# A streaming encoder layer on one core: the prompt's state products of the scan as fp32r passes with exchanged operands, and the norm products one weight half further on

## The chip, the core and the metric

The kernel runs on one core of a Trainium2 chip. The metric is the device time in microseconds of one execution; lower is better. Everything is fp32 in and out. The engines are called by their short names in the profile: PE is TensorE (matrix products; PEld is its weight load), DVE is VectorE, ACT is ScalarE, POOL is GpSimd and SP is SyncE, which issues most of the transfers.

## The reference, cut to what matters

One layer is computed for 256 frames of a new stream (the prompt) and for 8 running streams of 16 frames (the sample), 384 tokens together. The layer projects the normed input, runs a pooling branch and a Mamba-2 scan (SSD), merges them by gates, and ends with an MLP. The change lies in the scan, in the state that the scan leaves behind:

```python
y = jnp.einsum('btsgr,bsgrp->btgrp', cb[..., None] * decay, xdt)
y = y + jnp.einsum('btgn,bgrpn->btgrp', Cc, h) * jnp.exp(cum)[..., None]
last = cum[:, -1]
w_end = jnp.exp(last[:, None] - cum)
h = h * jnp.exp(last)[..., None, None] + jnp.einsum('bsgn,bsgr,bsgrp->bgrpn', Bc, w_end, xdt)
...
h = h * lax.rsqrt(jnp.mean(h * h, axis=-1, keepdims=True) + EPS)
```

There are 8 groups (g) of 8 heads of 64 channels, and a state of 128 per channel. For the prompt, whose state starts at zero, the state is a sum over all 256 frames of B times the weighted input: for each pair of heads, 128 channels by 128 states, summed over two blocks of 128 frames. It is an output (new_ssm_p). The last line is that of gated_rmsnorm, over a group's 512 channels.

## The kernel before, in words

**Arithmetic.** Most products are made of fp32r passes: each operand is split into a high part (a rounded copy, by ScalarE) and a low part (the rest, by VectorE), and three products, high by high, high by low and low by high, are summed in PSUM (mm3, L161; wsplit, L73). Products written on fp32 tiles show in the profile as two passes each.

**Weights.** The large projections run through flow (L121). Its list items holds weight halves: 1024 columns of a weight matrix, fetched by SP four halves ahead (fetch), split by ScalarE and VectorE two or three halves ahead (prep), and used in 24 products of 384 columns each (half, L166). Between halves stand calls, added by at(...), that do the scan's own work. Each engine executes its instructions in the order in which the program lists them.

**The work list.** Smaller work of VectorE and ScalarE is put in a list with a cost and a name (later, L88). After each half, work (L91) takes entries worth 2.6 from the front; need (L99) takes entries until the named ones are done.

**A block** (block, L592) belongs to half a group, so there are 16 of them plus a last call. It finishes the half group before it (old) and starts the next (new). For old, PE computes the outputs Y from the decayed products E (L603), adds the sample's part (L632), and computes the prompt's state pp: for each of two head pairs and two blocks of frames, one fp32 product with the weighted input xdw as weights and B (Bk) as the moving operand, 128 columns (L636). For new, PE computes the sample's input from its old state (yi, L623), transposes the inputs (trx, L643) and, in the first half of a group, B (trB, L648) and the products of C and B (cb, L651). The results lie in six PSUM banks, which are taken as others come free. VectorE then reads yi (yis, L655), Y (xs, L665) and trx (xdt, xdw, L676), ScalarE copies pp to pe (L667), and POOL stores it with two transfers (L669). In the first half of a group, ScalarE copies trB's prompt part to Bk (L684) and the sample's part is split into Bhl (L686, L687) and stored to b_scr (L688).

**The sample's state.** state_tasks (L717) splits the sample's third of xdw into xhl (L723, L724) and stores it to x_scr (L725). SP then loads the old state hs (L575) and reads b_scr and x_scr back in another layout: bst (L824) and xst (L833). update (L838) uses them for the su products, 256 columns in fp32r (L846).

**The norm.** gated_tasks (L729) sums the squares of a group in ssum and splits the sum into sh (ScalarE, L749) and sl (VectorE, L750). norm_mm (L791) sums them over the channels with two fp32r products bc_g (L795, L796) against ones, and puts the following steps of VectorE in the work list.

**The order by hand** (L869 to L907 for each group): B and C with the second update of the group before, three projections of x, a block, the fourth x, the transfers, z0, the first half of z1, an update, the second half of z1, norm_mm of the group before, z2, z3, a block, and a gate (gate_units, L553). At the end (L940 to L952) come the remaining gates with the last block, whose pp stands in the block, and the last norm. PE waits at a half whose weights are not split yet.

## Time and profile before

| what | value |
| --- | --- |
| three runs, median | 2798.02 us (2796.97 to 2801.68) |
| the profiled execution, its own time | 2799.5 us |
| its span, from the first to the last instruction | 2797.7 us |
| granted TensorE clock, mean | 0.998 |

The profile lists the engines' busy times, the chain that ended last, groups of instructions by line, waits and a timeline. In a timeline row stand the start in us from the span's start, the duration, the engine, the line, the operation, the tile written and the tiles read, the shapes, the count, and in brackets how long the engine had been idle before and what ended that. Matrix products overlap, so the pace of PE is read from start to start, not from a row's duration.

### The profile page before, as it was taken

To read this page: it belongs to the slowest core of one execution; us is meant where nothing else is said; L and a number is where in the kernel's file an instruction comes from. 1 tells how busy PE (TensorE), PEld (TensorE's weight loads), DVE (VectorE), ACT (ScalarE), POOL (GpSimd) and SP (SyncE) were. 2 spreads that over 40 slices of the span, in tenths; PEclk is the share of its full clock that TensorE was granted. 3 is DMA by queue.
4 is the path that set the end of the run, shared out by engine and by line. 5 is a ranking of instruction groups with operands and counts; after the bars stand their busy time and mean duration, and the time that the engine had idled before them with its cause. 6 is when DMAs were issued, how large, how long until landed. Compare 5 with 4: busy or idle time off the path is not lost.

```text
span 2797.7 us, 40260 instructions
## 1 busy us (share of the span) xinstructions
PE 2784.7 (100%) x15964; PEld 2656.5 (95%) x15964; DVE 1766.9 (63%) x2217; ACT 1323.5 (47%) x2076; POOL 191.0 (7%) x295
## 2 busy tenths in 40 slices
PE   9999999999999999999999999999999999999998
PEld 9999999999999999999999988999999999999997
DVE  8774334567667767667633334666767667676766
ACT  6443223555555554554422223545555555555553
POOL 0000000000000000001000000000111111111111
PEclk9999999999999999999999999999999999999999
DMA  6444445556556556555744454445666566666656
GB/s 223 134 134 139 138 141 171 191 170 216 193 181 209 197 183 208 199 184 186 263 158 155 151 200 132 153 165 185 179 162 166 162 161 163 176 177 186 183 125 249
DMA packets 161468, 492.89 MB, mean 176 GB/s; under 512 B 20032, under 2 KB 43392, under 8 KB 156416
## 3 DMA queue, kind: packets, MB, share of 16 engines
q1 hardware_dynamic: 133008, 406.07, 43.1%
q0 software_dynamic: 28128, 84.24, 12.6%
q8 instruction: 125, 2.05, 0.3%
q14 instruction: 63, 0.52, 0.1%
q10 hardware_dynamic: 144, 0.01, 0.0%
HBM read 412.35 MB, written 77.89 MB: 175 GB/s over the span
## 4 chain that ended last, share of the span: by engine, by line
PE 94%; DVE 2%; DMA 1%; ACT 1%; issue 1%; SPq 0%; DVEq 0%; ACTq 0%
PE pj_up L162 6%; PE pj_up L163 6%; PE pj_up L164 6%; PE pj_x L162 4%; PE pj_x L163 4%; PE pj_x L164 4%; PE wd L1410 3%; PE pj_sp L162 3%; PE wd L1411 3%; PE wd L1412 3%; PE pj_sp L164 3%; PE pj_sp L163 3%; PE pj_z L163 3%; PE pj_z L164 3%; PE pj_z L162 3%; PE t L1412 2%
## 5 line engine op out<-in xcount | busy, mean ns | idle before, releaser
L162 PE MATMUL pj_up<-x1h,wh_up 128*128 128x384 f32 x992 | 334.6, 337 | 0.0
L163 PE MATMUL pj_up<-x1l,wh_up 128*128 128x384 f32 x992 | 333.7, 336 | 0.0
L164 PE MATMUL pj_up<-x1h,wl_up 128*128 128x384 f32 x992 | 333.7, 336 | 0.0
L162 PE MATMUL pj_x<-xgh,wh_x 128*128 128x384 f32 x768 | 257.6, 335 | 0.0
L164 PE MATMUL pj_x<-xgh,wl_x 128*128 128x384 f32 x768 | 256.9, 335 | 0.0
L163 PE MATMUL pj_x<-xgl,wh_x 128*128 128x384 f32 x768 | 256.9, 335 | 0.0
L78 DVE TENSOR_TENSOR wl_wd<-raw,wh_wd 128x1024 fp32r<-128x1024 f32 x168 | 201.8, 1223 | 62.7 <-ACT wh_wd L77 59.0
L77 ACT ACTIVATE wh_wd<-raw 128x1024 fp32r<-128x1024 f32 x168 | 174.2, 1053 | 84.5 <-PE pj_up L163 42.1
L162 PEld LDWEIGHTS pj_up<-x1h,wh_up 128*128 128x128 f32 x992 | 186.9, 188 | 4.5
L163 PEld LDWEIGHTS pj_up<-x1l,wh_up 128*128 128x128 f32 x992 | 186.9, 188 | 4.5
L164 PEld LDWEIGHTS pj_up<-x1h,wl_up 128*128 128x128 f32 x992 | 186.9, 188 | 0.0
L164 PE MATMUL pj_z<-xgh,wl_z 128*128 128x384 f32 x512 | 171.3, 335 | 0.0
L162 PE MATMUL pj_z<-xgh,wh_z 128*128 128x384 f32 x512 | 171.3, 335 | 0.0
L163 PE MATMUL pj_z<-xgl,wh_z 128*128 128x384 f32 x512 | 171.3, 335 | 0.0
L162 PE MATMUL pj_sp<-abh,wh_sp 128*128 128x384 f32 x512 | 171.2, 334 | 0.0
L164 PE MATMUL pj_sp<-abh,wl_sp 128*128 128x384 f32 x512 | 171.2, 334 | 0.0
L163 PE MATMUL pj_sp<-abl,wh_sp 128*128 128x384 f32 x512 | 171.2, 334 | 0.0
L78 DVE TENSOR_TENSOR wl_sp<-w_sp,wh_sp 128x1024 fp32r<-128x1024 f32 x64 | 78.4, 1226 | 110.7 <-ACT wh_sp L77 110.7
L162 PEld LDWEIGHTS pj_x<-xgh,wh_x 128*128 128x128 f32 x768 | 144.3, 188 | 0.0
L163 PEld LDWEIGHTS pj_x<-xgl,wh_x 128*128 128x128 f32 x768 | 144.3, 188 | 0.0
L164 PEld LDWEIGHTS pj_x<-xgh,wl_x 128*128 128x128 f32 x768 | 144.2, 188 | 0.0
L78 DVE TENSOR_TENSOR wl_x<-w_x,wh_x 128x1024 fp32r<-128x1024 f32 x72 | 87.4, 1221 | 81.3 <-ACT wh_x L77 81.3
(388 smaller groups left out, 7094.2 us busy)
## 6 DMA issues: line engine op xcount, KB each, us to landing
w_up<-w_up SPq DMA_DIRECT2D x126, 512.0 KB, 4.6
raw<-w_down SPq DMA_DIRECT2D x112, 512.0 KB, 7.1
w_x<-w_in SPq DMA_DIRECT2D x96, 512.0 KB, 4.0
w_z<-w_in SPq DMA_DIRECT2D x64, 512.0 KB, 4.5
w_sp<-w_ssd SPq DMA_DIRECT2D x64, 512.0 KB, 4.7
acc_scr<-ev POOLq DMA_DIRECT2D x126, 256.0 KB, 4.4
w_ga<-w_in SPq DMA_DIRECT2D x32, 512.0 KB, 3.4
w_pp<-w_pp SPq DMA_DIRECT2D x32, 512.0 KB, 3.4
```

What stands on the lines that cost most here:

```text
L77: s.activation(h, w, AF.Copy)
L78: v.tensor_tensor(l, w, h.bitcast(F32), ALU.subtract)
L162: te.matmul(out, wh, xh, start=first, stop=False)
L163: te.matmul(out, wh, xl, start=False, stop=False)
L164: return te.matmul(out, wl, xh, start=False, stop=last)
L1410: te.matmul(o, ah, wh[:, c], start=first, stop=False)
L1411: te.matmul(o, ah, wl[:, c], start=False, stop=False)
L1412: te.matmul(o, al, wh[:, c], start=False, stop=fin)
```

## The change

The state products pp are no longer four fp32 products but two sets of three fp32r passes, with the operands exchanged: B is the weight, split into high and low, and the weighted input is the moving operand, for two head pairs at once (256 columns in two runs of 128). They run ahead of Y in the block, while the banks are asked for in the old order: Y, yi, pp. For that, Bk holds the high and the low part of all three thirds of B, and xhl those of all three thirds of the weighted input; the splits of Bhl and of the sample's third alone are gone. The store to x_scr becomes two transfers, one per part. The state is stored with one transfer of 256 columns in place of two of 128, in another layout that the host transposes.

The last state is taken out of the last block: its sample part is split where it was, its prompt part two weight halves later, and its products, copy and store follow after one more half, just before the last norm.

norm_mm of the other groups moves from the front of z2 to between its two halves.

Among the buffers, the copy pe uses the gates' buffer (tag gbt), of which there is now one instead of two until the tail, when the next phase's pool gives two; ms uses the buffers of the convolution (tag cacc). The scan's row of the constant table has a tile and a transfer of its own on POOL's queue (the table's other part shrinks by 408 columns), nrm moves to another pool, and two paddings change.

```diff
@@ -328,10 +328,13 @@
         half(early[4], 1, p4[1], xg)
     pha.close()
 
-    small.tile([P, 88], F32, name="pad_small")
+    small.tile([P, 80], F32, name="pad_small")
+    nrm = small.tile([P, 32], F32, name="nrm")
     tok = small.tile([P, 11, NH], F32, name="tok")
     decb = small.tile([P, NH, NB], F32, name="decb")
     with tc.tile_pool(name="phc", bufs=1, reuse_waits="tile") as pc, tc.tile_pool(name="phc2", bufs=2, reuse_waits="tile") as pc2:
+        scan = pc.tile([NH, T], F32, name="scan")
+        gp.dma_start(scan, io["cst"][:NH, C_SCAN : C_SCAN + T])
         bufs = []
         for i in range(2):
             b = pc.tile([P, 519], F32, name=f"pbuf{i}")
...
@@ -436,7 +439,7 @@
             v.scalar_tensor_tensor(out=dt, in0=q, scalar=2.0, in1=raw, op0=ALU.mult, op1=ALU.add)
             dta, we, dtw = n64("dta"), n64("we"), n64("dtw")
             v.tensor_scalar(dta, dt, nA, -1.0, ALU.mult, ALU.mult)
-            v.tensor_tensor_scan(cum, cst2[:NH, C_SCAN - C_MASK : C_SCAN - C_MASK + T], dta, 0.0, ALU.mult, ALU.add)
+            v.tensor_tensor_scan(cum, scan, dta, 0.0, ALU.mult, ALU.add)
             sy.dma_start(cum_scr, cum)
             nb = n64("nb")
             tot = pb.tile([NH, 1], F32, name="tot")
...
@@ -552,7 +554,10 @@
 
     def gate_units(n):
         def post(ps):
-            t = small.tile([P, T], F32, tag="gbt", name=f"gbt{n}", bufs=2)
+            if "pe1" in held:
+                t = held["pe1"].tile([P, T], F32, tag="gbt", name=f"gbt{n}", bufs=2)
+            else:
+                t = small.tile([P, T], F32, tag="gbt", name=f"gbt{n}", bufs=1)
             v.tensor_tensor(t, ps, rstd, ALU.mult)
             s.activation(t, t, AF.Sigmoid)
             gp.dma_start(gb_scr[n], t)
...
@@ -589,15 +594,32 @@
             ALU.mult,
         )
 
+    def state(g, hf, pp):
+        need(f"xhl{g}_{hf}")
+        d = S[g]
+        for b in range(2):
+            bh, bl = (d["Bk"][:, i, b, :] for i in range(2))
+            xh, xl = (d["xhl"][0][:, i, :, b, :] for i in range(2))
+            mm3(pp[:, : 2 * P].rearrange("p (j q) -> p j q", j=2), bh, bl, xh, xl, b == 0, b == 1)
+        return pp
+
+    def state_out(g, hf, pp):
+        pe = small.tile([P, T], F32, tag="gbt", name=f"pe{g}_{hf}", bufs=1)[:, : 2 * P]
+        s.copy(pe, pp[:, : 2 * P])
+        gp.dma_start(io["new_ssm_p"][g * 2 + hf], pe)
+
     def block(old, new):
         Y = []
         if old:
             g, hf = old
             need(f"E{g}_{hf * 2}", f"E{g}_{hf * 2 + 1}")
             d = S[g]
-            for j in (hf * 2, hf * 2 + 1):
-                y = sstile(f"Y{g}_{j}")
-                Y.append(y)
+            Y = [sstile(f"Y{g}_{j}") for j in (hf * 2, hf * 2 + 1)]
+            if new:
+                yi = sstile(f"yi{new[0]}_{new[1]}")
+                pp = sstile(f"pp{g}_{hf}")
+                state(g, hf, pp)
+            for j, y in zip((hf * 2, hf * 2 + 1), Y):
                 for sb, e0, c0, n in ((0, 0, 0, TP), (1, TP, P, P), (2, T, TP, P)):
                     for hh in range(2):
                         te.matmul(
...
@@ -616,7 +638,8 @@
                 need(f"x{32 + g2}", f"x{40 + g2}")
             need(f"x{g2 * 4 + j0}", f"x{g2 * 4 + j0 + 1}")
             hs = d2["hs"][h2]
-            yi = sstile(f"yi{g2}_{h2}")
+            if not old:
+                yi = sstile(f"yi{g2}_{h2}")
             for j2 in range(2):
                 for c in range(4):
                     for r in range(2):
...
@@ -630,10 +653,6 @@
         if old:
             for y, j2 in zip(Y, range(2)):
                 te.matmul(y[:, TP:T], d["yis"][hf][:, j2 * P : j2 * P + P], ident, start=False, stop=True, skip_group_check=True)
-            pp = sstile(f"pp{g}_{hf}")
-            for j2 in range(2):
-                for b in range(2):
-                    te.matmul(pp[:, j2 * P : j2 * P + P], d["xdw"][hf][:, j2, b, :], d["Bk"][:, b, :], start=b == 0, stop=b == 1)
         trx = []
         if new:
             for j in (j0, j0 + 1):
...
@@ -663,10 +682,8 @@
                 x = d["xs"][j]
                 i = V_DSK + g * 4 + j
                 v.scalar_tensor_tensor(out=x, in0=x, scalar=vec[:, i : i + 1], in1=y[:, :T], op0=ALU.mult, op1=ALU.add)
-            pe = pd.tile([P, 2 * P], F32, tag="pe", name=f"pe{g}_{hf}", bufs=1)
-            s.copy(pe, pp[:, : 2 * P])
-            for j2 in range(2):
-                gp.dma_start(io["new_ssm_p"][g * 4 + hf * 2 + j2], pe[:, j2 * P : j2 * P + P])
+            if new:
+                state_out(g, hf, pp)
         if new:
             xdw = d2["xdw"][h2] = pd.tile([P, 2, 3, P], F32, tag="xdw", name=f"xdw{g2}_{h2}", bufs=1)
             for j2, tr in enumerate(trx):
...
@@ -680,12 +697,11 @@
                         ALU.mult,
                     )
             if h2 == 0:
-                Bk = d2["Bk"] = pd.tile([P, 2, P], F32, tag="Bk", name=f"Bk{g2}", bufs=1)
-                s.copy(Bk.rearrange("p b n -> p (b n)"), trB[:, :TP])
-                Bhl = pd.tile([P, 2, P], F32R, tag="Bhl", name=f"Bhl{g2}", bufs=1)
-                s.activation(Bhl[:, 0, :], trB[:, TP:T], AF.Copy)
-                v.tensor_tensor(Bhl[:, 1, :], trB[:, TP:T], Bhl[:, 0, :].bitcast(F32), ALU.subtract)
-                sy.dma_start(b_scr[g2], Bhl.bitcast(F32))
+                Bk = d2["Bk"] = pd.tile([P, 2, 3, P], F32R, tag="Bk", name=f"Bk{g2}", bufs=1)
+                tb = trB[:, :T].rearrange("p (b n) -> p b n", b=3)
+                s.activation(Bk[:, 0], tb, AF.Copy)
+                v.tensor_tensor(Bk[:, 1], tb, Bk[:, 0].bitcast(F32), ALU.subtract)
+                sy.dma_start(b_scr[g2], Bk[:, :, 2, :].bitcast(F32))
                 cbm = d2["cbm"] = pd.tile([P, 512], F32, tag="cbm", name=f"cbm{g2}", bufs=1)
                 v.tensor_tensor(cbm, cb, cst2[:, :512], ALU.mult)
         if new:
...
@@ -717,14 +733,22 @@
     def state_tasks(g, hf):
         d = S[g]
 
-        def parts():
-            xhl = pd.tile([P, 2, 2, P], F32R, tag="xhl", name=f"xhl{g}_{hf}", bufs=1)
-            x = d["xdw"][hf][:, :, 2, :]
-            s.activation(xhl[:, 0], x, AF.Copy)
-            v.tensor_tensor(xhl[:, 1], x, xhl[:, 0].bitcast(F32), ALU.subtract)
-            sy.dma_start(x_scr[g * 2 + hf], xhl.bitcast(F32))
-
-        later(0.5, f"xhl{g}_{hf}", parts)
+        def parts(b):
+            if "xhl" not in d or d["xhl"][1] != hf:
+                d["xhl"] = pd.tile([P, 2, 2, 3, P], F32R, tag="xhl", name=f"xhl{g}_{hf}", bufs=1), hf
+            xhl = d["xhl"][0]
+            x = d["xdw"][hf][:, :, b, :]
+            s.activation(xhl[:, 0, :, b, :], x, AF.Copy)
+            v.tensor_tensor(xhl[:, 1, :, b, :], x, xhl[:, 0, :, b, :].bitcast(F32), ALU.subtract)
+            if b.stop == 3:
+                for i in range(2):
+                    sy.dma_start(x_scr[g * 2 + hf][:, i], xhl[:, i, :, 2, :].bitcast(F32))
+
+        if (g, hf) != (G - 1, 1):
+            later(0.5, f"xhl{g}_{hf}", lambda: parts(slice(0, 3)))
+            return
+        later(0.5, f"xhl{g}_{hf}", lambda: parts(slice(2, 3)))
+        held["parts"] = lambda: parts(slice(0, 2))
 
     def gated_tasks(g, hf):
         d = S[g]
...
@@ -794,7 +818,7 @@
         bc = sstile(f"bc_g{g}")[:, :T]
         te.matmul(bc, onesr, d["sh"], start=True, stop=False)
         te.matmul(bc, onesr, d["sl"], start=False, stop=True)
-        ms = pd.tile([P, T], F32, tag="ms", name=f"ms_g{g}", bufs=1)
+        ms = pd.tile([P, T], F32, tag="cacc", name=f"ms_g{g}")
         y = pd.tile([P, T], F32, tag="ssum", name=f"nwy_g{g}", bufs=1)
         a = pd.tile([P, T], F32, tag="ysq", name=f"nwa_g{g}", bufs=1)
 
...
@@ -893,9 +917,11 @@
         items += u[:1]
         at(update, g, 0)
         items += u[1:]
+        u = z_units(g, 2)
+        items += u[:1]
         if g:
             at(norm_mm, g - 1)
-        items += z_units(g, 2)
+        items += u[1:]
         u = z_units(g, 3)
         items += u[:1]
         at(cbc_load, g, 1)
...
@@ -945,7 +971,10 @@
     items += tail_[4:5]
     at(block, (G - 1, 1), None)
     at(narrow)
-    items += tail_[5:8]
+    items += tail_[5:7]
+    at(lambda: held["parts"]())
+    items += tail_[7:8]
+    at(lambda: state_out(G - 1, 1, state(G - 1, 1, sstile(f"pp{G - 1}_1"))))
     at(norm_mm, G - 1)
     items += tail_[8:11]
     at(branch_open)
```

More of the change, by code (lines that the diff above doesn't have):

```diff
@@ L228, in build @@
     rstd = small.tile([P, T], F32, name="rstd")
-    cst2 = small.tile([P, C_END - C_MASK], F32, name="cst2")
+    cst2 = small.tile([P, C_SCAN - C_MASK], F32, name="cst2")
     xg, xr = [None] * KD, [None] * KD
@@ L308, in build @@
         sy.dma_start(cst[:, :C_MASK], io["cst"][:, :C_MASK])
-        sy.dma_start(cst2, io["cst"][:, C_MASK:])
+        sy.dma_start(cst2, io["cst"][:, C_MASK:C_SCAN])
         f4 = [wfetch(win[5, q], f"p4_{q}") for q in range(2)]
@@ L508, in build @@
     s.activation(onesr, ones, AF.Copy)
-    nrm = pd1.tile([P, 32], F32, name="nrm")
     v.tensor_scalar(nrm, vec[:, V_NRM : V_NRM + 32], -1.0 / 8192.0, None, ALU.mult)
-    pd1.tile([P, 64], F32, name="pad_phd")
+    pd1.tile([P, 96], F32, name="pad_phd")
     seg = lambda a: a.rearrange("p (b t) -> p b t", b=24)
-    ncv = [0]
+    ncv, held = [0], {}
     def proj_units(ui, name, post):
@@ L907, in build @@
                 items += gate_units(gates.pop(0))
-    ab, ms_, held = [], [], {}
+    ab, ms_ = [], []
     AR = 7
@@ L1684 @@
         "new_conv": (P, 48, 9, 3),
-        "new_ssm_p": (32, P, P),
+        "new_ssm_p": (16, P, 2 * P),
         "new_ssm_s": (16, P, NB, 2 * P),
@@ L1697 @@
     nconv = r["new_conv"].transpose(2, 3, 1, 0).reshape(9, 3, 6144)
+    nsp = r["new_ssm_p"].reshape(16, P, 2, P).transpose(0, 2, 3, 1)
     nss = r["new_ssm_s"].reshape(16, P, NB, 4, 64).transpose(2, 0, 3, 4, 1).reshape(1, NB, NH, 64, P)
@@ L1704 @@
         c(nconv[:1].reshape(1, 1, 3, 6144)),
-        c(r["new_ssm_p"].reshape(1, 1, NH, 64, P)),
+        c(nsp.reshape(1, 1, NH, 64, P)),
         c(npool[1:].reshape(1, NB, 15, DM)),
```

## The prediction, made before the changed kernel ran

> **What bounds the kernel now.** I read the page first, for the engines' busy time and the chain that ended last, and then the windows view for the stretch from 490 to 1362 us, in which the scan's blocks lie.
>
> ```profile
> PE 2784.7 (100%) x15964; PEld 2656.5 (95%) x15964; DVE 1766.9 (63%) x2217; ACT 1323.5 (47%) x2076; POOL 191.0 (7%) x295
> PE 94%; DVE 2%; DMA 1%; ACT 1%; issue 1%; SPq 0%; DVEq 0%; ACTq 0%
> 490.00:1362.00 872.00, 871.30 (x5786) 854.65 (x5785) 619.79 (x877) 471.93 (x919) 52.41 (x96) 1.00 0.59 198
> ```
>
> The reader is to see that TensorE (PE) is the bound, over the whole span and in the changed stretch: busy 871.30 of 872.00 us, at a granted clock of 1.00. VectorE has 619.79 and ScalarE 471.93, so there is room beside PE, but both run in order and feed PE its weights. A microsecond taken from PE's stream comes off the end if PE is fed as before. I therefore count PE time from start to start, then ask which cover gets thinner.
>
> The timeline of PE, block of old group 0 and new group 1:
>
> ```profile
> 593.90 1.96 PE L603 MATMUL Y<-E,xdt 128*64 128x256 f32 x24
> ...
> 597.38 1.06 PE L636 MATMUL pp<-Bk,xdw 128*128 128x128 f32 x8
> 598.27 0.82 PE L643 MATMUL trx<-cst,xs 128*128 128x128 f32 x6
> ...
> 599.26 1.04 PE L651 MATMUL cb<-xs,xs 128*128 128x256 f32 x6
> 600.05 0.42 PE L162 MATMUL pj_x<-xgh,wh_x 128*128 128x384 f32 x1
> ```
>
> From Y's start to the next weight half are 6.15 us with no gap. The state products pp hold PE from 597.38 to 598.27, 0.89 us: four fp32 products, seen as eight passes.
>
> **State products: the new price.** The nearest row is the sample's update su: fp32r, 256 columns, other weights each time, as in the six new products.
>
> ```profile
> 516.04 1.11 PE L846 MATMUL su<-xst,bst 128*128 128x256 f32 x8
> 516.99 0.34 PE L162 MATMUL pj_z<-xgh,wh_z 128*128 128x384 f32 x1
> ```
>
> Eight take 0.95 us, 0.119 each; six take 0.71. Each of the 16 blocks saves 0.89 - 0.71 = 0.18, together **2.8 us**. No switch between fp32r and fp32 is added: the new products stand right behind an fp32r weight half, ahead of Y, and in the last block between two halves. The su row reads its moving operand in one run, the change reads two runs of 128 columns; no row here has that. Bounds: at no price 0.119 each; at the pace of pp (0.89 for 8 x 128 columns, 0.22 for 256) 1.33 a block, 0.44 more than before, a loss of 7.0 in all. I take su's row, the same type and width.
>
> The Trainium skill, TensorE: Matmul & The Clock Gate, section Back-to-back issue gap, gives N/2.4 + 2.5 ns for a product standing alone on a warm clock, which is 109 ns for 256 columns; six would be 0.65 and the saving 3.8. The trace's 0.119 is longer and decides.
>
> **Norm products.** The timeline of PE at the norms of groups 0, 1 and 2 (their last weight product, two norm products, next half), and group 6, where nothing waits; below them who ended the waits, from the view of the tile:
>
> ```profile
> 625.89 0.34 PE L164 MATMUL pj_z<-xgh,wl_z 128*128 128x384 f32 x1
> 627.03 0.34 PE L162 MATMUL pj_z<-xgh,wh_z 128*128 128x384 f32 x1
> ...
> 731.76 0.34 PE L164 MATMUL pj_z<-xgh,wl_z 128*128 128x384 f32 x1
> 733.38 0.34 PE L162 MATMUL pj_z<-xgh,wh_z 128*128 128x384 f32 x1
> ...
> 838.12 0.34 PE L164 MATMUL pj_z<-xgh,wl_z 128*128 128x384 f32 x1
> 838.88 0.34 PE L162 MATMUL pj_z<-xgh,wh_z 128*128 128x384 f32 x1
> ...
> 1259.45 0.34 PE L164 MATMUL pj_z<-xgh,wl_z 128*128 128x384 f32 x1
> 1259.98 0.33 PE L162 MATMUL pj_z<-xgh,wh_z 128*128 128x384 f32 x1
> ...
>   ACT sh L749: 1.4, 3
>   DVE sl L750: 1.1, 3
> ```
>
> The quiet case takes 0.53 us. Groups 0, 1 and 2 take 1.14, 1.62 and 0.76, so they wait 0.61, 1.09 and 0.23, **1.9 us**, for the two halves sh and sl of the sum of squares. The later groups wait hardly at all: the whole view has 2.5 us, part of it overlapped. Half a step later, PE has one more weight half to run, 24 products or about 4.16 us (627.03 to 631.19, below). sl would have to come over 4 us later than now to be waited for.
>
> Gross gain: 2.8 + 1.9 = **4.7 us**.
>
> **What is late next: the weights behind the norm.** In the timelines of VectorE and PE, the split that the half after next needs:
>
> ```profile
> 626.14 0.56 DVE L750 TENSOR_TENSOR sl<-ssum,sh 128x384 fp32r<-128x384 f32 x1 [0.59 <-ACT sh L749]
> 627.75 1.22 DVE L118 TENSOR_TENSOR wl_z<-w_z,wh_z 128x1024 fp32r<-128x1024 f32 x1
> 631.19 0.34 PE L162 MATMUL pj_z<-xgh,wh_z 128*128 128x384 f32 x1
> ...
> 734.10 1.22 DVE L78 TENSOR_TENSOR wl_z<-w_z,wh_z 128x1024 fp32r<-128x1024 f32 x1
> 737.54 0.34 PE L162 MATMUL pj_z<-xgh,wh_z 128*128 128x384 f32 x1
> ```
>
> The split ends at 628.97 and PE needs it at 631.19: a slack of 2.22, the same in group 1 (735.32 to 737.54). PE waited at the norm just before, so without that wait the slack is 2.22 - 0.61 = 1.6 in group 0, 2.22 - 1.09 = 1.1 in group 1, 2.0 in group 2, and about 2.4 in the other four.
>
> How much later does that split come? Its weights were issued by SP behind the block's own transfers, and SP waits there for xhl:
>
> ```profile
> 603.28 0.33 SPq L725 DMA_DIRECT2D x_scr<-xhl  x1
> 603.71 0.37 SPq L575 DMA_DIRECT2D hs<-ssm  x1
> 604.13 0.44 SPq L70 DMA_DIRECT2D w_z<-w_in  x1
> ...
> 613.98 2.69 SPq L833 DMA_DIRECT2D xst<-x_scr  x4
> 616.72 0.91 SPq L70 DMA_DIRECT2D w_z<-w_in  x2
> ```
>
> The x_scr store becomes two, one more issue of about 0.42 (603.71 to 604.13), and xhl is split over three times the columns. The view of groups by shape, over 490 to 1362 us, prices that:
>
> ```profile
> L724 DVE TENSOR_TENSOR xhl<-xdw,xhl 128x256 fp32r<-128x256 f32 x16 | 6.7, 416 | 0.0
> L687 DVE TENSOR_TENSOR Bhl<-trB,Bhl 128x128 fp32r<-128x128 f32 x8 | 2.2, 278 | 0.0
> ```
>
> Between xhl's 0.42 for 256 columns and the weight split's 1.22 for 1024, 768 columns come to 0.95, so +0.53. Bhl goes from 128 to 384 columns, 0.28 to the 0.56 of sl above, +0.28. With the issue, the chain is about **1.2 us later**. Against slacks of 1.6, 1.1, 2.0 and 2.4 that costs group 1 some 0.1; I take 0.3 for all groups. ScalarE's added columns (Bk and the high half of xhl) run while VectorE works through the block and cost nothing.
>
> **Other cover that gets thinner.** The old pp stood between Y's last products and trB and cb, which take banks that this block sets free. In the block of group 2:
>
> ```profile
> 704.13 1.13 DVE L665 SCALAR_TENSOR_TENSOR xs<-xs,vec,Y 128x384 f32<-128x384 f32 x2
> 704.44 0.35 ACT L667 COPY pe<-pp 128x256 f32<-128x256 f32 x1
> 705.13 1.04 PE L651 MATMUL cb<-xs,xs 128*128 128x256 f32 x6
> ```
>
> cb began at 705.13 while the second xs product ran to 705.26, so cb doesn't wait for that one; the copy of pp ended at 704.79. In the new order cb comes 0.18 earlier, at 704.95. The copy keeps its place on ScalarE, behind a SiLU, so 0.16 is left: price 0. With the bank of the second xs product it would be some 0.35 in each of seven blocks, 2.5.
>
> At the end, the copy of the last state shares one buffer with the gates and waits on ScalarE, an in-order engine, until gate 10's store has landed; behind it stands the split that PE needs two halves later.
>
> ```profile
> 1319.72 0.56 DVE L556 TENSOR_TENSOR gbt<-pj_gb,rstd 128x384 f32<-128x384 f32 x1
> 1321.13 0.54 POOL L558 DMA_DIRECT2D gb_scr<-gbt  x1 [7.73 <-ACT gbt L557]
> DMA to landing us min/median/max: 2.1/4.3/5.4
> ```
>
> Landing at the median, 1325.4, plus copy 0.4, ScalarE's split 1.05 and VectorE's 1.22 makes 1328.1; PE starts that half at about 1328.2 (two halves of 4.16 after 1319.88). So 0 to 1.1 us, once; I take 0.3. The late halves of the last xhl are split while PE runs a whole half, price 0. The last state's 16th saving is in the sum. Moving nrm, the shorter constant table, the scan row on POOL's queue and one state store in place of two lie beside PE's work in earlier stages or on POOL, busy 7%: price 0, and if the earlier stages are laid out otherwise, unknown by about 1 us either way.
>
> **Sum.** 2.8 + 1.9 - 0.3 - 0.3 = 4.1 us. The profiled execution took 2799.5 us, its span 2797.7 and 1.8 around it; it becomes 2795.4. The median of the three runs, 2798.02, lies 1.5 below the profiled one, so I predict **2794.0 us**. I call 0.2%, 5.6 us, what a measurement can tell from no change: below 2792.4 is faster, above 2803.6 slower.
>
> **Rivals.**
> - *Given back* (0.16). Bank order costs 2.5, or the chain is 2.5 us late in place of 1.2: then groups lose 0.9 + 1.4 + 0.5 + 4 x 0.1 = 3.2. For it: the slacks were read from one order of the work, and every block adds to them. Against: the issue and columns add up to 1.2. Time 2796 to 2797.
> - *Slower: the weights behind the norm* (0.13). If the chain from xhl over hs to the weights is d late, the loss is (d - 1.6) + (d - 1.1) + (d - 2.0) + 4 x (d - 2.4), positive parts only; at d = 2.7 it eats the 4.7, and at 4 it is 2.4 + 2.9 + 2.0 + 6.4 = 13.7: 2807. It decides at d above 3.5 for over 0.2%. For it: the store's runs shrink from 2 KB to 512 bytes, and hs, 1 MB, follows on the same queue. Against: xst, the reader of x_scr, is issued at 613.98, over ten microseconds after the store, so a slower landing is covered.
> - *The new passes run slow* (0.06): two-run moving operands at fp32's pace, +7.0 - 1.9: 2803. It is also the case that the change doesn't do what it says.
> - *More than forecast* (0.15). Products spaced by their columns alone, 256/384 of the 0.173 us between weight products (4.16/24), or 0.116, give 3.1; with 1.9 and no give-back 5.0, 2793.0, and scatter of 1 us in the median takes it under 2792.4. The Trainium skill's 109 ns would give 3.8 + 1.9 = 5.7: 2792.3.
> - Forecast (0.50): 2792.5 to 2796.
>
> DMA: Bandwidth & Descriptors, section Specifications, of the Trainium skill puts the least size for line rate at 512 bytes; by it the store's runs cost nothing. No row here shows such a store.
>
> **How the numbers follow.** Faster by over 0.2%: most of the "more" case and the forecast's edge, 0.20. Slower: the slow-weights case and half of the slow passes, 0.16. Within: 0.64. The range goes from 2790.5 (the "more" case less scatter) to 2803.0 (slow passes), leaving out the rest of the slower case.
>
> **What would show it.** Six state products from start to start in 0.71 us, ahead of Y, and the block at 5.97; norms with 0.53 in all groups; the split behind the norm 1.2 us later against the block's start, with PE waiting there 0.1 at most. Wrong would be: gaps before a weight half behind the norm, cb starting late, PE standing at the half after the last state.

## The result, and the profile after

The changed kernel takes **2803.68 us** (median of 9 runs, 2802.67 to 2808.46) against 2798.59 for the kernel before (9 runs): ratio 1.0021, 95% interval 1.0013 to 1.0030. The forecast was 2794.0 with a range to 2803.0, so it had the wrong sign, and the time lies 0.7 us beyond the range. The profiled execution took 2808.34 us and lies 4.7 above the median; the stages below are read from it, so their sums are those of this execution, 8.9 us over the profiled execution of the kernel before, and not of the medians, which lie 5.1 apart.

The page of the changed kernel, and the window of the scan's blocks:

```profile
PE 2786.7 (99%) x15932; PEld 2655.6 (95%) x15932; DVE 1777.7 (63%) x2218; ACT 1329.8 (47%) x2069; POOL 183.2 (7%) x280
490.00:1371.00 881.00, 873.95 (x5758) 855.71 (x5757) 629.49 (x876) 477.50 (x911) 42.92 (x80) 1.00 0.59 196
```

PE was busy in all but 0.70 us of that stretch before; now it stands for 7.05. The timeline of PE, first the new state products of the block of group 1 and what follows them, then the norm of group 1:

```profile
593.48 0.28 PE L162 MATMUL pp<-xhl,Bk 128*128 128x256 f32 x1
...
594.07 0.28 PE L164 MATMUL pp<-xhl,Bk 128*128 128x256 f32 x1
594.28 1.96 PE L625 MATMUL Y<-E,xdt 128*64 128x256 f32 x24
597.76 0.82 PE L662 MATMUL trx<-cst,xs 128*128 128x128 f32 x6
598.78 0.55 PE L667 MATMUL trB<-cst,xs 128*128 128x128 f32 x3 [0.20 <-DVE yis L674]
...
737.01 0.34 PE L819 MATMUL bc_g<-sh,onesr 128*128 128x384 f32 x1
737.18 0.34 PE L820 MATMUL bc_g<-sl,onesr 128*128 128x384 f32 x1
737.36 0.33 PE L162 MATMUL pj_z<-xgh,wh_z 128*128 128x384 f32 x1
```

What was to be gained is there. The six state products start 0.12 us apart; the last is 0.21 ahead of Y, because the switch from fp32r to fp32 (0.09) now stands behind them and no longer behind the weight half. The norm takes 0.35 us from its first product to the next half, with no gap. But trB, which followed the transposes of x after 0.66 us, now follows after 1.02 here. The waits of PE in the changed kernel, from 540 to 1290 us and from 1290 to 1400 us (us in total, times, longest):

```profile
PE trB L667 <- DVE yis L674: 5.3, 7, 1.8
...
PE pj_gb L164 <- DVE wl_gb L78: 0.9, 2, 0.4
PE pp L163 <- DVE xhl L742: 0.6, 1, 0.6
PE pj_sp L164 <- DVE wl_sp L78: 0.2, 1, 0.2
```

There are two new places: the transposes of B in every first half of a group, which wait for VectorE's yis, and the stretch behind the last block.

To add it up I compare the start of the same weight half in two traces; each column says by how much the difference to the kernel before grows in a stage (us, minus is a gain). "First-half blocks" are the seven with trB and cb, the half behind them included.

| stage | changed | e1 norm alone | e2 state alone | e4 tail | e5 taps | e6 taps, tail | e10 | e13 |
| --- | --- | --- | --- | --- | --- | --- | --- | --- |
| norms | -2.0 | -2.0 | +1.6 | -2.0 | -2.0 | -2.0 | -2.0 | -2.0 |
| eight second-half blocks | -1.5 | 0 | -1.5 | -1.5 | -1.5 | -1.5 | -1.5 | -1.5 |
| seven first-half blocks | **+9.2** | +0.5 | +3.5 | +6.8 | -0.7 | -0.9 | +6.8 | +1.9 |
| other halves of the scan | 0 | 0 | 0 | 0 | +1.9 | +1.5 | 0 | 0 |
| last block | -1.0 | +0.8 | -1.0 | -1.0 | -1.0 | -1.0 | -1.0 | -1.0 |
| last state | +1.6 | 0 | +0.7 | +0.7 | +1.3 | +0.7 | +0.7 | +0.7 |
| gates and the next loop | **+2.3** | 0 | +1.2 | 0 | +2.0 | 0 | +2.1 | +0.7 |

The first-half blocks would be 1.3 us shorter without waits (7 x 0.19, as in the other eight), so they lose some 10.5: 6.4 ahead of trB, 1.3 ahead of cb, the rest beside these, with 1.65 from a lower clock in one block (last section). Together the changed column is 8.6 of the 8.9 us by which the spans differ. Not all of it is the program's: e4 runs the same instructions up to the tail, and there the blocks lose 6.8 in place of 9.2, with waits of 5.6 and 1.3 and no lower clock. That is the scatter against which the waits of the other runs are to be held.

### The profile page after: what moved, and what is told of

The parts are those of the page before. It is cut to its first block, busy times and chain, and to the rows that moved or that the text cites. A ratio compares the mean times of both kernels' runs of the same rounds, so it can differ in the third digit from the quotient of the medians.

```text
span 2806.6 us, 40258 instructions
## 1 busy us (share of the span) xinstructions
PE 2786.7 (99%) x15932; PEld 2655.6 (95%) x15932; DVE 1777.7 (63%) x2218; ACT 1329.8 (47%) x2069; POOL 183.2 (7%) x280
## 4 chain that ended last, share of the span: by engine, by line
PE 39%; issue 34%; DVE 13%; ACT 6%; POOL 4%; DMA 3%; SPq 1%; POOLq 0%; DVEq 0%; ACTq 0%
POOL acc_scr L1407 3%; PE pj_sp L164 3%; PE pj_sp L163 3%; PE pj_sp L162 3%; DVE cacc L543 2%; PE pj_ga L164 2%; PE pj_ga L163 2%; PE pj_pp L164 2%; PE pj_pp L162 2%; PE pj_ga L162 2%; PE pj_pp L163 2%; PE wo L1111 2%; PE wo L1113 2%; PE wo L1112 2%; DVE wl_x L78 1%
## 5 line engine op out<-in xcount | busy, mean ns | idle before, releaser
L77 ACT ACTIVATE wh_wd<-raw 128x1024 fp32r<-128x1024 f32 x168 | 174.2, 1053 | 84.5 <-PE pj_up L163 42.1
```

Of the source, the lines that this page charges most:

```text
L77: s.activation(h, w, AF.Copy)
```

## The experiments

Three terms: the taps are the three multiply-adds of the convolution of one x tile on VectorE (L543); a round is what ScalarE and VectorE do for one half group; cover is the time between the end of a result and the moment at which another engine needs it.

Each block of times below: median, then that of the kernel before on the same chip, then the ratio with its interval. "Waits at trB and cb" are the seven gaps ahead of each, start to start, beyond the quiet 0.11. An execution scatters by about 2 us, so small edits are read from the traces.

### The two edits alone

e1 is the kernel before with norm_mm moved, e2 the changed kernel with it moved back:

```diff
+        u = z_units(g, 2)
+        items += u[:1]
         if g:
             at(norm_mm, g - 1)
-        items += z_units(g, 2)
+        items += u[1:]
```

> The kernel before with the norm products alone one weight half further; the state products stay fp32, behind the Y additions. Theory A (the loss of the change sits at the transposes of B, which take the bank of yi and so wait for VectorE's yis, and in the tail; both came with the state products, not with the norm): the three norm waits of 0.61, 1.09 and 0.24 us go and little is given back, 2796.7 us against 2798.6. Rival B (PE is paced by the weights or by VectorE's own chain, and whatever PE gains is waited for again at the next block): 2798.6, with new gaps ahead of the transposes of B as long as the norm waits were.

> The changed kernel with the norm products at their old place: the state products alone are changed. Theory A: the norm waits of 1.9 us come back, but PE then reaches the next block of a first half that much later, while VectorE's yis is where it was, so the waits ahead of the transposes of B in groups 2 and 3 shrink by up to as much: 2803.7 to 2804.7 us. Rival B (the state's loss is a price of its own, whatever PE's lead): 2805.6.

e1: 2797.62, before 2797.66, 0.9998 [0.9990, 1.0007]. Waits at trB and cb 0.3. The norm's 2.0 us are gained; 0.5 come back in one block, and 0.8 at the last, where the fp32 products of the last state come too early for a bank:

```profile
PE pp L636 <- DVE hs L850: 0.6, 1, 0.6
```

By the trace 0.7 us of the gain are left, which the time can't show.

e2: 2803.28, before 2797.66, 1.0019 [1.0010, 1.0028]; 0.4 under the range of theory A, 2.3 under rival B. The loss belongs to the state edit, and e2 shows its kind: in place of a gain the norms lose 1.6, the waits at trB and cb are 0.33 and 0.19 in every group, and the time is the changed kernel's. What PE doesn't wait for in one place it waits for in the other, so something else paces it.

### What trB waits for: VectorE's order

In the changed kernel, VectorE comes to yis only after the taps of the group's third x tile, which the block doesn't need. e3 holds them back until yis is issued:

```diff
+            if hold:
+                held["taps"] = taps
+                debt[0] -= 1.8
...
                 tok[:, 10, hd : hd + 4].unsqueeze(2).to_broadcast([P, 4, 64]),
                 ALU.mult,
             )
+            if "taps" in held:
+                held.pop("taps")()
```

e5 holds them back until the xs products and the copy of the last state are issued too:

```diff
             if new:
                 state_out(g, hf, pp)
+                if "taps" in held:
+                    held.pop("taps")()
```

> The changed kernel with one edit of VectorE's order: in the blocks of a first half the three taps of the group's third x tile, which the block does not need, stand behind yis instead of ahead of it. PE's order is the same. Theory A: yis ends about 0.45 us after PE's yi products, ahead of the transposes of x; the gaps between the transposes of x and of B (0.36, 1.35, 0.77, 0.77, 0.88, 1.98, 0.33 us, 6.4 in all) go to about nothing: 2803.7 - 6.4 = 2797.3 us. Rival B (VectorE and ScalarE are simply late; what is taken from one wait comes back at the next x half): 2801 to 2803. Rival C (another cause than yis, such as the bank of cb or the second xs): the gaps stay, 2803.7.

> The changed kernel with VectorE's three taps of the third x tile put behind yis and behind both xs products in the blocks of a first half, and so the copy of the last state ahead of that tile's silu on ScalarE. Moving them behind yis alone had moved PE's wait from the transposes of B to the scores (one bank later). Theory A2 (the wait is for whatever bank VectorE and ScalarE free behind those taps): both gaps go, PE does the block in its own 6.2 us, 0.5 to 2 us less per group than in the changed kernel: 2796.5 us. Rival B2 (the round of ScalarE and VectorE through one group has become longer than PE's, so PE waits in every group, wherever the order puts it): the gap turns up at the weight halves behind the block or at the next block, 2801 to 2804.

e3: 2805.82, before 2797.66, 1.0025 [1.0015, 1.0035]. My theory fell in the form that I had given it. The gap ahead of trB is gone in all seven blocks, and 10.3 us stand ahead of cb instead:

```profile
PE cb L674 <- DVE xs L690: 9.2, 7, 1.4
```

cb takes the bank of a Y, which is free once xs has read it, and xs now stood behind the taps. e5: 2798.15, before 2797.87, 1.0000 [0.9991, 1.0009]. With both readers ahead of the taps, the waits at trB and cb are 0.2. That is theory A2, but not wholly: 1.9 us come back at halves behind the blocks, the 0.5 below among them, as B2 had it.

```profile
PE su L876 <- DMA xst<-x_scr: 0.5, 1, 0.5
PE pj_z L164 <- DVE wl_z L118: 0.2, 1, 0.2
```

e12 is the control: the kernel before, with e1's norm and e5's order of the taps.

> The kernel before with the norm products one weight half further and the taps behind yis and the xs products, as in e5; the states stay fp32 with their narrow splits. If the taps' place is worth something only where VectorE is late (theory W), this is the norm alone: within 0.5 us of it by the trace, some 1 to 2 us under the kernel before, 2796.5 us. Rival (the order of the taps is a gain of its own, which hid the loss in e5 and e6): 2 us or more under the norm alone, 2794.5 us or less.

2797.20, before 2797.50, 1.0000 [0.9991, 1.0009]; its blocks are those of the kernel before to 0.01 us. The order is worth nothing where VectorE isn't late.

### Not the place of the products

e7 sets them back behind the Y additions:

```diff
-                state(g, hf, pp)
...
                 te.matmul(y[:, TP:T], d["yis"][hf][:, j2 * P : j2 * P + P], ident, start=False, stop=True, skip_group_check=True)
+            if new:
+                pp = sstile(f"pp{g}_{hf}")
+                state(g, hf, pp)
```

> The changed kernel with the state products (still fp32r with exchanged operands) back behind the Y additions in every block. Cover theory (the products' old place gave VectorE 0.8 us between the Y additions and the transposes of B): the seven waits shrink by up to 0.8 each, 2799 us. Theory B2 (in either place the products stand ahead of the transposes of B, and PE reaches these as early as now, so the place gives no cover): the waits stay, 2803.7, or up to 1.4 more for two more changes of type per block.

2802.59, before 2797.87, 1.0020 [1.0011, 1.0029]; waits 6.4 and 1.2, as in the changed kernel. The cover theory falls: in both places the products stand ahead of trB.

### The wider splits, engine by engine

Between two blocks ScalarE works without a gap and VectorE waits for it. ScalarE in the kernel before (L723 is the x split, L767 the table load ahead of the exponentials, L77 a weight split); then in the changed kernel, and VectorE there:

```profile
650.91 0.42 ACT L723 ACTIVATE xhl<-xdw 128x256 fp32r<-128x256 f32 x1 [1.24 <-DVE xdw L676]
651.35 1.28 ACT L767 ACT_TABLE_LOAD   x1
...
659.00 1.04 ACT L77 ACTIVATE wh_x<-w_x 128x1024 fp32r<-128x1024 f32 x1
```

```profile
651.57 0.85 ACT L741 ACTIVATE xhl<-xdw 128x768 fp32r<-128x768 f32 x1 [3.09 <-DVE xdw L693]
652.44 1.28 ACT L791 ACT_TABLE_LOAD   x1
...
660.10 1.04 ACT L77 ACTIVATE wh_x<-w_x 128x1024 fp32r<-128x1024 f32 x1
```

```profile
652.59 0.95 DVE L742 TENSOR_TENSOR xhl<-xdw,xhl 128x768 fp32r<-128x768 f32 x1
661.17 1.23 DVE L78 TENSOR_TENSOR wl_x<-w_x,wh_x 128x1024 fp32r<-128x1024 f32 x1 [7.63 <-ACT wh_x L77]
```

The split takes 0.85 us in place of 0.42 and everything behind it, table load, exponentials and weight split, follows at the old spacing: wh_x comes 1.10 us later (0.43 from the split, 0.66 from the round before), and VectorE, idle for 7.63 us, can't make it up. The next block shows where it lands. VectorE in the block of group 2, one row of the kernel before, then the changed kernel with PE's trB:

```profile
703.80 0.42 DVE L655 TENSOR_TENSOR yis<-yi,tok 128x256 f32<-128x256 f32 x1
...
703.06 1.93 DVE L543 SCALAR_TENSOR_TENSOR cacc<-cbuf,vec,cacc 128x384 f32<-128x384 f32 x3 [0.96 <-ACT cacc L538]
704.91 0.42 DVE L674 TENSOR_TENSOR yis<-yi,tok 128x256 f32<-128x256 f32 x1
705.24 1.13 DVE L684 SCALAR_TENSOR_TENSOR xs<-xs,vec,Y 128x384 f32<-128x384 f32 x2
705.38 0.55 PE L667 MATMUL trB<-cst,xs 128*128 128x128 f32 x3 [1.18 <-DVE yis L674]
```

yis starts at 704.91, at 703.80 before, and xs at 705.24, at 704.13 before: again 1.1 us. PE is there 0.7 us sooner, and trB, which takes yi's bank, waits 1.35. Four kernels say which part of the splits does it. Three of them leave out low parts in the states: e9 that of B, e10 those of B and the prompt's x, e13 that of the prompt's x. e9 has the new splits and fp32 products:

```diff
-            mm3(pp[:, : 2 * P].rearrange("p (j q) -> p j q", j=2), bh, bl, xh, xl, b == 0, b == 1)
+                te.matmul(pp[:, j2 * P : j2 * P + P], d["xdw"][hf][:, j2, b, :], d["Bk"][:, 0, b, :].bitcast(F32), start=b == 0, stop=b == 1)
```

e10 makes the low parts of x and B as narrow as before (the line of x):

```diff
-            v.tensor_tensor(xhl[:, 1, :, b, :], x, xhl[:, 0, :, b, :].bitcast(F32), ALU.subtract)
+                v.tensor_tensor(xhl[:, 1, :, 2, :], d["xdw"][hf][:, :, 2, :], xhl[:, 0, :, 2, :].bitcast(F32), ALU.subtract)
```

e13 makes ScalarE's part narrow and lets VectorE copy the prompt's high part, so that VectorE has about as much to do as in the changed kernel; e16 keeps the low part at full width besides, and has both edits of the tail (e4 below):

```diff
-            s.activation(xhl[:, 0, :, b, :], x, AF.Copy)
+                s.activation(xhl[:, 0, :, 2, :], d["xdw"][hf][:, :, 2, :], AF.Copy)
+                v.tensor_copy(xhl[:, 0, :, 0:2, :], d["xdw"][hf][:, :, 0:2, :])
```

> The changed kernel with its whole wider splitting left in, but the state products as eight fp32 products at the same place (they use the high part of B alone, so the low part of B is left out of the states, and rows and columns come out exchanged). Theory W (the wider splits on ScalarE and VectorE make the round late; PE's own gain in the products adds only its 0.1 us): the seven waits ahead of the transposes of B stay, 5 to 7 us in all, and the block is 0.1 to 0.2 us longer: 2804 us. Rival P (PE arrives early because of the faster products, the splits cost nothing): the waits go to 1 us or less, 2799 us.

> The changed kernel with VectorE's low parts as narrow as before the change: the low parts of the prompt's x and B are neither made nor used (the products read the high parts in their place, so both low parts are left out of the states); ScalarE's high parts are as wide as in the change, and PE's work is the same. Theory V (VectorE's 0.5 us more per half and 0.27 per B are most of it): the waits go from 6.4 to 2 us or less, 2799 us. Theory S (ScalarE's 0.43 us more ahead of the exponentials sets the round): the waits stay above 4 us, 2802 or more.

> The changed kernel with ScalarE's x split as narrow as before the change (256 columns): the prompt's high part is a copy on VectorE, and its low part is neither made nor used (so it is left out of the states); VectorE has as much to do as in the change, in one instruction more per half. Theory S (ScalarE's 0.43 us ahead of the exponentials sets the round back): the waits ahead of the transposes of B go from 6.4 to 2 us or less, 2799 us. Rival (the two engines hand the work to each other, and time taken from one alone does not shorten the round; or the cause is neither split): the waits stay above 4 us, 2802 or more.

> The whole computation, with the prompt's high part of the x split copied by VectorE (0.42 us in e13) instead of ScalarE, and both edits of the tail; the taps stay where they are. Theory S (ScalarE alone set the round back): the waits ahead of the transposes of B stay at 1 to 2 us in all and the tail's 3 us are gone: 2795.5 us, some 2.3 under the kernel before. Rival (VectorE's low part of 768 columns, which e13 had left out, brings the waits back): 4 us or more of waits, 2798 us or more.

| run | time, before | ratio [interval] | waits at trB + cb |
| --- | --- | --- | --- |
| e9 | 2804.60, 2797.50 | 1.0028 [1.0016, 1.0039] | 5.6 + 1.3 |
| e10 | 2803.28, 2797.50 | 1.0021 [1.0012, 1.0030] | 5.6 + 1.3 |
| e13 | 2799.56, 2797.80 | 1.0008 [0.9999, 1.0017] | 1.1 + 1.2 |
| e16 | 2799.93, 2797.18 | 1.0008 [0.9999, 1.0017] | 3.2 + 1.3 |

The waits of PE in e10 and in e13:

```profile
PE trB L667 <- DVE yis L674: 4.5, 7, 1.0
```

```profile
PE trB L667 <- DVE yis L674: 0.7, 1, 0.7
```

e9: with the old arithmetic and the new splits the loss is all there, so it is the splits. e10: taking VectorE's extra columns away leaves the waits, 5.6 + 1.3 as in e4, which has the changed kernel's blocks; theory V falls. e13: taking ScalarE's away leaves 1.1 of the wait at trB, a fifth of e4's. But e16, whose low part is made at full width, is at 3.2 + 1.3, where 2 at most was expected for trB: it gives VectorE 0.42 us more per half than the changed kernel has, and with ScalarE relieved that costs something too. ScalarE sets the round first, VectorE is close behind.

e8 makes the prompt's part of the split later, behind the decay masks, and e14 gives it to GpSimd:

```diff
             decay_masks(g2, h2)
+            later(0.9, f"xhp{g2}_{h2}", held["parts"])
```

```diff
+                gp.tensor_copy(xhl[:, 0, :, 0:2, :], d["xdw"][hf][:, :, 0:2, :])
+                gp.tensor_tensor(xhl[:, 1, :, 0:2, :], d["xdw"][hf][:, :, 0:2, :], xhl[:, 0, :, 0:2, :].bitcast(F32), ALU.subtract)
```

> The changed kernel with the x split in two: the part of the short sequences is made where it was before the change, the prompt's part behind the decay masks, out of the way of the exponentials. Theory B2 in its first form (the split of 768 columns ahead of the exponentials, 0.85 us for 0.42 on ScalarE and some 0.5 more on VectorE, sets the whole round back by 0.4 to 0.6 us per half group): the waits ahead of the transposes of B go to a third, about 2 us in all, 2799.5 us. Rival (the work counts, not its place; 15 more instructions on each of the two engines): 2803 to 2805.

> The changed kernel with both prompt parts of the x split made by GpSimd (two instructions per half), the part of the short sequences as before the change on ScalarE and VectorE. Theory W: the waits go to 1 us or less in all and the block of a first half to 6.1 to 6.4 us: 2803.7 - 6.5 = 2797 to 2798 us. Rival (GpSimd's work slows VectorE's by as much, or the cause is neither split): the waits stay above 4 us, 2802 or more.

e8: 2809.14, before 2797.87, 1.0040 [1.0026, 1.0054], waits 9.3 + 1.2: the rival, and worse. The columns cost in this place too, and two parts take longer than one: 0.42 + 0.61 in place of 0.85 on ScalarE, 0.41 + 0.68 in place of 0.95 on VectorE. The Trainium skill, Perfetto Trace Analysis, section Optimizing Scalar/DVE Operations, says that where these engines cause bubbles without being saturated, breaking instructions up may finish work sooner; here breaking the split up and making the larger part later did the opposite. e14: 2803.39, before 2797.80, 1.0021 [1.0011, 1.0030], waits 3.3 + 1.3: about half are gone, where 1 at most was expected, and the time is the rival's. What VectorE has to pay for GpSimd is in the groups of the changed kernel and of e14 (mean ns of one behind the busy time; in e14 the mean mixes splits of 1.22 us with some of 2.29, see the last section):

```profile
L118 DVE TENSOR_TENSOR wl_z<-w_z,wh_z 128x1024 fp32r<-128x1024 f32 x14 | 17.1, 1218 | 0.0
```

```profile
L118 DVE TENSOR_TENSOR wl_z<-w_z,wh_z 128x1024 fp32r<-128x1024 f32 x14 | 21.3, 1525 | 0.0
L746 POOL TENSOR_TENSOR xhl<-xdw,xhl 128x512 fp32r<-128x512 f32 x14 | 18.0, 1288 | 1.2
```

### The tail, and the versions that the runs point to

ScalarE and VectorE behind the last state, in the changed kernel:

```profile
1331.99 0.37 ACT L608 COPY pe<-pp 128x256 f32<-128x256 f32 x1 [4.85 <-DMA gb_scr<-gbt]
1332.26 2.01 ACT L77 ACTIVATE wh_gb<-w_gb 128x1024 fp32r<-128x1024 f32 x2
...
1333.36 1.22 DVE L78 TENSOR_TENSOR wl_gb<-w_gb,wh_gb 128x1024 fp32r<-128x1024 f32 x1 [5.91 <-ACT wh_gb L77]
```

The copy takes the gates' only buffer, waits 4.85 us for the gate's store, and holds up two weight splits. e4 gives it a buffer and makes the last x split sooner; e6 is that with e5's order of the taps:

```diff
+        if (g, hf) == (G - 1, 1):
+            pe = pd.tile([P, 2 * P], F32, tag="yis", name=f"pe{g}_{hf}")
...
     items += tail_[2:4]
+    at(lambda: held["parts"]())
     at(update, G - 1, 1)
```

> The changed kernel with two edits of the tail: the last state's copy goes to a buffer of its own (one that yis no longer needs) instead of the gates' single one, and the early parts of the last x split are made three weight halves sooner. Theory A: ScalarE no longer stands 4.85 us for the gate's store, the weight halves behind it are split in time, and the last state's first products lose their wait of 0.8 us: 0.8 + 2.3 = 3.1 us less, 2800.6 us; the gaps ahead of the transposes of B stay at 6.4 us in all. Rival (the waits behind the last state are those of late loads, or the sp loop takes back what is gained): 2803 or more.

> The same order of the taps together with the two edits of the tail (own buffer for the last state, its early split sooner). Theory A2: 3.1 us less than the taps alone, 2793.4 us, which would beat both kernels. Rival B2: 2798 to 2801.

e4: 2803.06, before 2797.66, 1.0017 [1.0009, 1.0026]. By the trace the tail's 2.3 us and the last state's 0.9 are gone, 3.2 as expected. The time doesn't show it: against the kernel before, the median lies 5.4 above, the changed kernel's 5.1 on its own chip, so it is the rival's. With the taps in order it does: e6, 2795.75, before 2797.87, 0.9993 [0.9984, 1.0002], 2.4 us under e5; 2793.4 was expected, and 1.5 us stand at halves between the blocks. The copy in e6 follows the gate without a wait:

```profile
1318.04 0.53 ACT L566 ACTIVATE gbt<-gbt 128x384 f32<-128x384 f32 x1 [1.95 <-DVE gbt L565]
1318.47 0.35 ACT L615 COPY pe<-pp 128x256 f32<-128x256 f32 x1
```

e15 is e6 with GpSimd's split, e17 is e6 with e16's:

> GpSimd's split with the order of the taps and both edits of the tail: the candidate for the best. Theory W: as e6 (2795.75 us, 2.1 us under the kernel before) or up to 0.5 us better, since the weight halves behind the blocks are split sooner: 2795.3 us. Rival (GpSimd slows VectorE): 2797 us or more.

> The same with the order of the taps as in e5 on top. Theory S: no waits at the banks, and the weight halves behind the blocks sooner than in e6: 2794.8 us, some 3 under the kernel before. Rival: as e6, 2795.8 us or more, since the waits were already gone there.

e15: 2795.26, before 2797.80, 0.9992 [0.9983, 1.0001]. e17: 2795.95, before 2797.18, 0.9996 [0.9987, 1.0005]; e15 as expected, e17 as its rival. Their blocks have no wait left, 6.06 us each, but 2.4 and 2.6 us come back at the halves between, and 1.7 and 1.0 of the norm's 2.0. So three versions (e6, e15, e17) lie 6 to 8 us below the changed kernel (measured against the kernel before in each case) and 1 to 2.5 below the kernel before, the latter within what these runs can tell from no change.

## Why the prediction was wrong, step by step

- **State products, 0.89 to 0.71, 2.8 us: right.** From the last weight product ahead of a block to the next half, every second-half block is 0.19 shorter, and the first-half blocks are too where nothing waits (6.24 in e17, 6.42 before). The two-run moving operand costs nothing: 0.12 us a pass. Only the block by itself takes 6.06 and not 5.97, since the switch of type moved into it.
- **Norm waits, 1.9 us: right.** 2.0 by the traces, 0.35 us in each group.
- **Weights behind the norm, 0.3: hidden.** PE has no wait at those halves in the changed kernel, having stood ahead of trB before. Where the blocks hardly wait, the halves behind the norm take longer, by 0.7 us in e5 and e6, 1.5 in e17 and 2.1 in e15, in part through the split wl_z that the prediction named. The rival that was slower through them fell: nothing near its 13.7 appears.
- **"ScalarE's added columns (Bk and the high half of xhl) run while VectorE works through the block and cost nothing": the step that failed.** I looked for their cover in the block and not behind it. There ScalarE has some 8 us of exponentials and then the weight split without a gap, VectorE idle beside it. The 0.43 us go through to the next block whole, where yis stands behind the taps. e9 shows that the splits cost the waits by themselves, e13 that ScalarE's part is the larger. Bk is not that part: on ScalarE one split of 0.49 us stands for a copy of 0.37 and a split of 0.28.
- **"Other cover that gets thinner", price 0: wrong at the same point.** I priced the banks of the copy and of xs and never that of yi, which trB takes. In the kernel before, yis ended at 704.22 and trB began at 704.80: 0.6 us of cover, which the 1.1 us and PE's lead used up. The rival "given back" named banks and a longer chain, with 2.5 to 3.2 us; the blocks lost 10.5.
- **Tail, 0.3 for the buffer and 0 for the late halves: too small.** The mechanism of the buffer was the one forecast; I took it to cost 0 to 1.1 once. The copy waited, two splits came late, and four halves lost 2.3 in all. The late halves of xhl cost 0.8: they stood on ScalarE behind the weight split of 1322.08.
- **Sum.** In e17, where the blocks don't wait, the changed products, the blocks and the last state give -1.5 - 1.3 - 1.0 + 0.7, and with the norm's 2.0 that is 5.1; I had 4.7. The gain was right, though e17 gives 3.6 of it back at the halves between the blocks. The changed kernel's profile lost 13.7 us against it: 10.5 in the first-half blocks, where two engines with 53% and 37% idle time were late, and 3.2 in the tail. That the time lies only 0.7 us beyond the range is luck: its upper end came from slow passes, which the runs rule out.

Open: what makes e5, e6, e15 and e17 wait at the halves between blocks (1.9, 1.5, 4.1 and 3.6 us, the norm's halves included), with several releasers of 0.2 to 0.6, wasn't taken apart. The way from the weight split at 661.17 to the taps at 703.06 was not followed row by row; it is e13 that ties the two ends together. Nor is the share of VectorE's part certain, since e16's waits lie in the last three of its seven blocks only.

## What to carry to other kernels

An engine's share of idle time says nothing about a chain that runs through it without a gap: before a few tenths of a microsecond are added to ScalarE or VectorE at no price, follow the chain from that instruction to the next point where PE waits for it, and compare with the cover there. Where PE waits for a bank, list every bank that the block takes and the instruction that frees it; an independent job that stands ahead of that instruction in the same queue is the first thing to move, with all the other readers of banks, not one. A buffer that is shared to make room ties two engines to a store's landing.

## What the runs showed of the hardware

- **The clock answers to a short stand.** In the changed kernel PE stood 2.09 us ahead of trB in the block of group 6, and the granted clock then fell to 0.50. The windows view, one us each (the third number from the end is the clock, the one behind the length PE's busy time):

```profile
1129.00:1130.00 1.00, 0.00 (x0) 0.00 (x0) 0.93 (x2) 0.00 (x0) 0.00 (x0) 1.00 0.00 0
1130.00:1131.00 1.00, 0.31 (x3) 0.31 (x3) 1.00 (x3) 0.66 (x2) 0.00 (x0) 1.00 0.00 0
1131.00:1132.00 1.00, 0.97 (x5) 0.65 (x3) 1.00 (x3) 0.94 (x3) 0.49 (x1) 0.66 0.00 0
1132.00:1133.00 1.00, 1.00 (x7) 0.91 (x5) 1.00 (x4) 0.71 (x1) 0.04 (x1) 0.50 0.37 131
1133.00:1134.00 1.00, 1.00 (x5) 1.00 (x5) 1.00 (x4) 0.42 (x1) 0.00 (x0) 0.50 0.01 0
1134.00:1135.00 1.00, 1.00 (x5) 1.00 (x5) 1.00 (x3) 0.98 (x2) 0.00 (x0) 0.64 0.00 0
1135.00:1136.00 1.00, 1.00 (x8) 1.00 (x7) 1.00 (x2) 0.99 (x2) 0.00 (x0) 1.00 1.04 164
```

  It cost 1.65 us. Gaps of 2.19 us in e8 and 2.27 in e9 did the same; one of 2.12 in e7 and one of 2.01 in e8 did not (all from start to start). A wait of some two microseconds can so cost nearly twice its length. The length alone doesn't decide: in every trace the clock records change in steps of 3.413 us, counted from the first of them, and the step ahead of the fall held 1.85 us without PE in the changed kernel, 1.92 in e8 and 2.02 in e9, but 1.72 in e7 and 1.53 in e8's shorter gap, both of which reached over the end of a step. This is no threshold, since behind the scan steps with 1.31 us were followed by a fall too (before, changed, e15) and one with 1.30 was not (e1). The Trainium skill, TensorE: Matmul & The Clock Gate, section Part 1: The HAM clock gate (the "warmup" mystery), has half rate after an idle window of about 3.4 us and full rate again after a busy one of about 3.4. The half rate and the 3.4 us of recovery agree (1131.3 to 1134.7, worked out from the shares 0.66 and 0.64 of the first and last slice); the idle time was shorter here.
- **GpSimd beside VectorE can hold VectorE up.** In each first half of e14, one weight split of VectorE ran beside GpSimd's subtraction and took 2.29 us in place of 1.22; in the second halves one ran beside GpSimd's copy and took 1.22, while the copy took 1.73 in place of 0.61:

```profile
707.45 0.61 POOL L745 CAST xhl<-xdw 128x512 fp32r<-128x512 f32 x1 [1.71 <-issue]
708.14 1.28 POOL L746 TENSOR_TENSOR xhl<-xdw,xhl 128x512 fp32r<-128x512 f32 x1
708.22 2.29 DVE L78 TENSOR_TENSOR wl_z<-w_z,wh_z 128x1024 fp32r<-128x1024 f32 x1
...
650.84 1.21 DVE L78 TENSOR_TENSOR wl_x<-w_x,wh_x 128x1024 fp32r<-128x1024 f32 x1
651.13 1.73 POOL L745 CAST xhl<-xdw 128x512 fp32r<-128x512 f32 x1 [2.08 <-issue]
```

  The Trainium skill, Perfetto Trace Analysis, in the section named above, warns that work moved between these two might not help, since they share a port; the rows agree.
- **A cast alone is cheap on VectorE.** 512 columns took 0.42 us in e13, as long as the subtraction of 256:

```profile
651.67 0.42 DVE L743 TENSOR_TENSOR xhl<-xdw,xhl 128x256 fp32r<-128x256 f32 x1
652.00 0.42 DVE L745 CAST xhl<-xdw 128x512 fp32r<-128x512 f32 x1
```
